# Token order, block products for one more feed-forward unit, and the order of wide and narrow matmuls in a two-layer encoder

## The chip, the cores and the metric

The kernel runs on one core of one Trainium2 chip. The metric is device microseconds of one execution; lower is better. The engines are named as in the profile: PE (TensorE, matmuls), PEld (its weight loads), DVE (VectorE), ACT (ScalarE), POOL (GpSimd) and SP (SyncE, which issues most DMAs). The kernel was run three times, and one further execution was profiled.

## What is computed

Two layers of an encoder over 512 tokens (a grid of 8 rows by 64 columns) of width 1024. Each layer has a mixer (neighbourhood attention and grouped-query attention), a cross attention to 256 memory tokens, and the feed-forward part that the change is about:

```python
def conv_ffn(h, w_up, conv_w, conv_b, w_down):
    u = h @ w_up                                    # (512, 1024) @ (1024, 2 * 2816)
    up = jnp.pad(u, ((0, 0), (1, 1), (0, 0)))
    u = up[:, :-2] * conv_w[0] + up[:, 1:-1] * conv_w[1] + up[:, 2:] * conv_w[2] + conv_b
    gate, val = jnp.split(u, 2, axis=-1)
    return (jax.nn.silu(gate) * val) @ w_down

def reference(x, mem, ...):
    for l in range(DEPTH):                          # DEPTH = 2
        x = x + hybrid_mixer(rms_norm(x, norm_mix[l]), ...)
        x = x + memory_cross_attention(rms_norm(x, norm_mem_q[l]), rms_norm(mem, norm_mem_kv[l]), ...)
        x = x + conv_ffn(rms_norm(x, norm_ffn[l]), w_up[l], conv_w[l], conv_b[l], w_down[l])
    return rms_norm(x, norm_final)
```

The convolution runs over neighbouring positions in the reference's order of tokens, in which token 64 r + c is row r, column c of the grid.

## The kernel before

**Layout.** Activations lie transposed: 128 of the 1024 features on the partitions, 512 tokens along the free dimension, in eight chunks `xT[c]`. Tokens are kept column by column: token 8 c + r is row r, column c, so that a window of the neighbourhood attention is a run of tokens. The neighbour in the convolution then lies 8 places away, except at the seam from one row of the grid to the next.

**Precision.** Every float32 operand is split into a rounded part `hi` and a remainder `lo`, and a product of two is three matmuls (`mm3`, called by `gemm_T`): hi by hi, hi by lo, lo by hi. ACT makes `hi` and POOL or DVE `lo`, of the activations as of the weights (`emit_split`).

**Feed-forward.** A unit is 128 columns of gate and 128 of value; there are 22 per layer. A plain unit (`up_project`) is two sides of 8 chunks by 3 matmuls of 512 columns: 48 wide matmuls. The first `PLAIN` = 6 units are plain. The others (`up_forms`) use a scheme of seven block products in place of eight: the weights of gate and value as a 2 by 2 block matrix over halves of the features, the tokens as two halves of 256. The sums and differences of weight blocks are made ahead by DMAs that add in DRAM (`make_form`, for the groups of `SHARES_OF_FORMS`), those of tokens once per layer: `scale_tokens` writes the scaled tokens to SBUF, `token_sums` forms t1 to t4 from them, `split_form` rounds each form into hi and lo. In one product (`product`) each of four chunks takes two matmuls:

```python
PE.matmul(bank, wh[:, i], both, start=start and k == 0, stop=False, skip_group_check=True)
PE.matmul(bank[:, halves[0]], wl[:, i], both[:, halves[0]], start=False, stop=k == 3, skip_group_check=True)
```

The first is wide, 512 columns: 256 tokens of `hi` and beside them 256 of `lo`. The second is narrow: the 256 of `hi`. A unit of this kind is 28 wide and 28 narrow matmuls in three PSUM banks (`mm`, `tr`, `sc`); the halves of a bank are added afterwards on DVE, ACT and POOL. So plain units are bound to the operands `ffn.ops`, the others to `xform`; t3, b22 and t4 are written over `ffn.hi` and `ffn.lo` once the plain units have read them.

**After the matmuls** of a unit, `convolve` applies the three taps (ACT the middle one, DVE the two others, each in two pieces because of the seam), silu and the product, and `split_psum` rounds the result, `acts[j]`. `GROUPS` puts the 22 units into four groups. The down projection of a group (`down`) has 8 rows of 3 matmuls per unit; its rows are placed between the products of the next group's units by `sequence`, one or two per unit. The last group's is done by `down_closing` (layer 0) or `down_last` (layer 1, with the final norm and the output).

**Order.** The program is recorded first, and a planner (`Order`) then fixes the order on PE, DVE, ACT and POOL from its own table of costs, with a search by a fixed seed. PE may be moved ahead of the written order where a matmul's operands are planned to be late. SP keeps the written order. Buffers are handed out from pools: 21 general tiles `r`, 14 temporaries `t`, PSUM banks `mm` 4, `sc` 2, `tr` 2, and two large tiles `xg` for a normalised operand.

In the rows of the profile the sides of plain units are 24 matmuls of 128x512 in a row into `mm` or `sc` with `xg` as input; a product is eight matmuls, 128x512 and 128x256 in turn, with `r` or `xg` as the tokens' form; a row of the down projection is 15 or 18 matmuls of 128x512 into `mm` with `r` as input. A few matmul records can be missing from a trace.

Of the kernel before, what the change touches and what calls it, by code (L numbers as in the profile page):

```python
# [19 lines left out]
P = 128  # L20
S = 512
# [4 lines left out]
NB = S // P  # L26
KC = D // P
# [5 lines left out]
GROUPS = [(0, 6), (6, 6), (12, 5), (17, 5)]  # L33
# [5 lines left out]
PLAIN = 6  # L39
SHARES_OF_FORMS = [(6, 4), (10, 4), (14, 4), (18, 4)]  # L40
# [50 lines left out]
class Counted(Free):  # L91
# [4 lines left out]
    def matmul(self, out, lhsT, rhs, **k):  # L96
        n = 1
        for d in rhs.shape[1:]:
            n *= d
        self.ns += max(107.0, (n + 32) / 2.4)  # L100
        return self.engine.matmul(out, lhsT, rhs, **k)  # L101

# [581 lines left out]
def encoder_kernel(ctx: ExitStack, tc: tile.TileContext, t: dict, out: bass.AP):  # L684
# [151 lines left out]
    def sequence():  # L836
# [4 lines left out]
        for g, (j0, nj) in enumerate(GROUPS):  # L841
            row = 0
            for j in range(j0, j0 + nj):
                to = 0 if g == 0 else min(KC, 2 * (j - j0) + 1) if j < j0 + nj - 1 else KC
                rows, row = range(row, to), to
                if j < PLAIN:
                    yield "up", j, None
                    continue
# [149 lines left out]
    def row_rep(rstd, n, tag, bufs, copy):  # L998

        pr = row_bank(rstd, n)  # L1000
        rep = tpool.tile([P, n * P], F32, tag=tag, name=nm(tag), bufs=bufs)
        copy(rep, pr[:, : n * P])
        return rep, pr[:, : n * P]

    class Norm:
# [11 lines left out]
        def close(self, c, pm):  # L1017


            DVE.tensor_add(pm, pm, xT[c])  # L1020
            DVE.tensor_copy(xT[c], pm)
            self.operand(c, src=pm)
            self.square(c)

        def operand(self, c, act=ACT, src=None, dve=DVE, hi_only=False, lo_only=False):
# [3 lines left out]
            e = None if lo_only else act.activation(hi, src, AF.Copy, scale=g)  # L1029
# [44 lines left out]
        def spread(self, copy=ACT.copy):  # L1074
            self.rep, self.psum = row_rep(self.rstd, self.n // P, "rep", 1, copy)
# [122 lines left out]
    for l in range(DEPTH):  # L1198
# [641 lines left out]
        ffn = nn  # L1840
        acts = {}

        def up_project(j, side):
            pm = ps_s() if side else ps_mm()
            gemm_T(pm, get_w(("up", j, side)), ffn.ops, range(KC), 0, KC - 1)
            return pm

        def up_first():
# [3 lines left out]
            for side in range(2):  # L1852
                ws.append(get_w(("up", 0, side)))
                us.append(ps_mm())
                gemm_T(us[side], ws[side], ffn.ops, range(KC - 1), 0, KC - 1)
            for side in range(2):
                gemm_T(us[side], ws[side], ffn.ops, [KC - 1], 0, KC - 1)
# [16 lines left out]
        def convolve(j, us):  # L1874
            cs = []
            for side in range(2):
# [31 lines left out]
        def scale_tokens():  # L1908
# [3 lines left out]
            for c in range(KC):  # L1912
                DVE.scalar_tensor_tensor(xn[c // 2][:, c % 2], xT[c], ffn.gain(c), ffn.psum, op0=ALU.mult, op1=ALU.mult)

        def token_sums():


            for name, a, b in (("t1", (0, 1), (0, 0)), ("t2", (1, 1), "t1"), ("t3", (1, 1), (0, 1)), ("t4", (1, 0), "t2")):
                raw = raw_forms[name] = rtile((4, HALF), F32)
                for i in range(2):  # L1920
                    k = slice(2 * i, 2 * i + 2)
                    one, other = quarter(*a)[i], raw_forms[b][:, k] if isinstance(b, str) else quarter(*b)[i]
                    if name == "t4":
                        POOL.tensor_add(raw[:, k], one, other)
                    elif name == "t2":
                        DVE.tensor_sub(raw[:, k], other, one)
                    else:
                        (POOL if name == "t3" else DVE).tensor_sub(raw[:, k], one, other)

        def split_form(name, where=None):  # L1930
# [4 lines left out]
            for i, v in enumerate(place):  # L1935
                hi, lo = (v[:, :, half] for half in halves)
                src = quarter(*direct[name])[i] if name in direct else raw_forms[name][:, 2 * i : 2 * i + 2]
                if name in ("t1", "t4"):
                    ACT.mul(hi, src, -1.0)
                    DVE.scalar_tensor_tensor(lo, src, -1.0, f(hi), op0=ALU.mult, op1=ALU.subtract)  # L1940
                else:
                    ACT.copy(hi, src)
# [281 lines left out]
```

## Time and profile before

| | |
|---|---|
| median of 3 runs | 1304.17 us (1303.88 to 1304.24) |
| the profiled execution | 1304.26 us, of which the span from first to last instruction 1302.5 |
| ACT, share of the span | 60% |
| POOL, share of the span | 66% |
| weight loads on PE, share of the span | 84% |
| HBM read, written | 218.45 MB, 69.21 MB |

A page of the profile shows for each engine the time in which it was busy, and the chain of work that ended last, followed back from the last instruction. A row of that chain is a start, a duration, an engine, the tile written, the line and a count. The list of waits has, for an engine and a line, what ended its idle time, the total, the times and the longest. A row of the timeline is a start, the time until the end, an engine, a line, an operation with output and inputs, its size and a count; since matmuls are pipelined, each lasts longer than the distance from its start to the next one's, and that distance is what it costs. Rows of groups end with busy time and mean duration (ns), then idle time before. Rows of a stretch have, per engine (PE, PEld, DVE, ACT, POOL), busy time and count, then the granted clock, the DMA share and GB/s.

### The profile page before, as it was taken

Reading aid. Unit: us, or ns where it says so; the run is one execution under the profiler, and the core shown is the slowest. Engines: PE = TensorE matmul, PEld = TensorE weight load, DVE = VectorE, ACT = ScalarE, POOL = GpSimd, SP = SyncE. Lnnn points to the kernel's source line nnn. Section 1 sums busy time; section 2 is a strip of 40 time slices with the busy share of each in tenths; the row PEclk is TensorE's granted clock in tenths of the full one; section 3 lists DMA queues with packets and bytes.
Section 4 is the critical chain, followed back from the end, with each engine's and each line's share of the span. In section 5 each row is a group of like instructions: output and inputs, shape, how many; then the busy total and the mean of one; then the engine's idle time right before and its main releaser. Section 6 shows DMA issues by size and latency. Waiting matters only on the chain.

```text
span 1302.5 us, 19581 instructions
## 1 busy us (share of the span) xinstructions
PE 1292.3 (99%) x6699; PEld 1096.4 (84%) x6699; DVE 916.0 (70%) x1869; ACT 776.6 (60%) x1463; POOL 857.7 (66%) x650
## 2 busy tenths in 40 slices
PE   9999999999999999999999999999999999999997
PEld 8888888888888888888888888888888888888887
DVE  6559877665996685676735698776759966666675
ACT  6667866565564554454636687775645545545454
POOL 3657966728667776776746579766466766767673
PEclk9999999999999999999999999999999999999999
DMA  9734599597787789687555435986872454555541
GB/s 289 211 108 121 160 262 203 168 211 199 186 192 204 207 230 234 189 234 212 157 152 172 144 84 185 253 191 214 186 170 85 130 158 134 163 157 150 149 138 65
DMA packets 287426, 229.68 MB, mean 176 GB/s; under 512 B 7648, under 2 KB 243680, under 8 KB 287328
## 3 DMA queue, kind: packets, MB, share of 16 engines
q1 hardware_dynamic: 270016, 194.49, 49.7%
q0 software_dynamic: 16896, 33.56, 14.6%
q8 instruction: 53, 0.87, 0.3%
q10 hardware_dynamic: 416, 0.39, 0.1%
q14 instruction: 45, 0.37, 0.1%
HBM read 218.45 MB, written 69.21 MB: 221 GB/s over the span
## 4 chain that ended last, share of the span: by engine, by line
PE 95%; DVE 3%; ACT 1%; issue 1%; POOL 0%; POOLq 0%; DVEq 0%; ACTq 0%
PE mm L101 69%; PE sc L101 18%; PE tr L101 4%; PE tr L1586 2%; PE tr L1431 1%; PE tr L1780 1%; DVE t L1891 0%; DVE r L1080 0%; DVE sc L1403 0%; PE tr L1501 0%; DVE r L1129 0%; DVE t L1456 0%; DVE t L1489 0%; ACT r L1079 0%; ACT t L1409 0%
## 5 line engine op out<-in xcount | busy, mean ns | idle before, releaser
L790 POOL TENSOR_TENSOR lo<-raw,hi 128x512 fp32r<-128x512 f32 (+3 forms) x325 | 567.0, 1761 | 280.6 <-ACT hi L789 224.1
L789 ACT CAST hi<-raw 128x1024 fp32r<-128x1024 f32 (+3 forms) x361 | 287.8, 814 | 274.4 <-issue 71.3
L101 PE MATMUL mm<-r,hi 128*128 128x512 f32 (+1 forms) x1344 | 432.8, 390 | 0.0
L101 PEld LDWEIGHTS mm<-r,hi 128*128 128x128 f32 x1344 | 246.4, 188 | 49.8
L101 PE MATMUL mm<-r,lo 128*128 128x512 f32 (+1 forms) x832 | 286.5, 347 | 0.0
L101 PE MATMUL mm<-xg,hi 128*128 128x512 f32 x800 | 262.2, 394 | 0.6 <-DVE t L1963 0.6
L101 PE MATMUL mm<-xg,lo 128*128 128x512 f32 (+1 forms) x528 | 177.9, 337 | 0.0
L101 PEld LDWEIGHTS mm<-r,lo 128*128 128x128 f32 x832 | 156.4, 188 | 22.6 <-POOL lo L790 0.5
L101 PEld LDWEIGHTS mm<-xg,hi 128*128 128x128 f32 x800 | 148.6, 188 | 31.9 <-DVE t L1963 1.0
L101 PE MATMUL sc<-xg,hi 128*128 128x512 f32 x352 | 116.3, 395 | 0.0
L101 PE MATMUL mm<-hi,xg 128*128 128x512 f32 (+1 forms) x384 | 111.2, 360 | 0.0
L101 PEld LDWEIGHTS mm<-xg,lo 128*128 128x128 f32 x528 | 99.4, 188 | 12.2
L1086 POOL TENSOR_SCALAR t<-t,s 128x512 f32<-128x512 f32 (+1 forms) x112 | 67.2, 623 | 45.6 <-DVE s L1570 22.2
L101 PE MATMUL sc<-xg,lo 128*128 128x256 f32 (+1 forms) x240 | 79.4, 332 | 0.0
L1982 POOL TENSOR_TENSOR t<-t 128x256 f32<-128x256 f32 x32 | 42.4, 1324 | 56.1 <-ACT t L1981 55.2
L101 PEld LDWEIGHTS sc<-xg,hi 128*128 128x128 f32 x352 | 66.1, 189 | 14.5 <-ACT xg L78 0.4
L101 PEld LDWEIGHTS mm<-hi,xg 128*128 128x128 f32 x384 | 68.0, 189 | 9.1 <-DVE r L1280 0.2
L101 PE MATMUL sc<-r,r 128*128 128x256 f32 (+1 forms) x352 | 74.4, 330 | 0.0
L1989 DVE TENSOR_TENSOR sc<-mm,t 128x256 f32<-128x256 f32 x32 | 13.8, 433 | 79.2 <-ACT t L1988 79.2
L101 PE MATMUL sc<-r,hi 128*128 128x512 f32 x192 | 68.7, 398 | 0.0
L101 PE MATMUL mm<-lo,xg 128*128 128x512 f32 (+1 forms) x192 | 68.6, 357 | 0.0
L790 DVE TENSOR_TENSOR lo<-raw,hi 128x1024 fp32r<-128x1024 f32 (+1 forms) x36 | 44.2, 1229 | 33.8 <-ACT hi L789 33.5
(222 smaller groups left out, 2438.3 us busy)
## 6 DMA issues: line engine op xcount, KB each, us to landing
raw<-in_w_up SPq DMA_DIRECT2D x56, 512.0 KB, 4.5
dr_sums<-in_w_up SPq DMA_DIRECT2D x16, 1024.0 KB, 8.0
dr_diffs<-in_w_up SPq DMA_DIRECT2D x16, 1024.0 KB, 7.6
raw<-dr_sums SPq DMA_DIRECT2D x32, 512.0 KB, 4.1
raw<-dr_diffs SPq DMA_DIRECT2D x32, 512.0 KB, 4.1
raw<-in_w_in SPq DMA_DIRECT2D x25, 512.0 KB, 4.8
raw<-in_w_down SPq DMA_DIRECT2D x32, 384.0 KB, 3.7
raw<-in_w_mem_kv SPq DMA_DIRECT2D x16, 512.0 KB, 4.4
```

The costliest lines, as they stand in the source:

```text
L101: return self.engine.matmul(out, lhsT, rhs, **k)
L789: act.copy(hi[:, k], raw[:, k])
L790: (POOL if eng[0] == "P" else DVE).tensor_sub(lo[:, k], raw[:, k], f(hi)[:, k])
L1086: eng.tensor_scalar(e, e, sums[:, col : col + 1], 1.0, op0=ALU.mult, op1=ALU.mult)
L1431: PE.transpose(tr[:, (2 * i + c) * P : (2 * i + c + 1) * P], es[j][:, i, c * P : (c + 1) * P], ident)
L1586: PE.transpose(tr[:, k * P : (k + 1) * P], es[j][:, k * P : (k + 1) * P], ident)
L1780: PE.transpose(tr[:, (2 * c + i) * P : (2 * c + i + 1) * P], e[:, i, c * P : (c + 1) * P], ident)
L1982: POOL.tensor_add(vc, vc, u2)
L1989: DVE.tensor_add(ch, ah, l4)
```

## The change

It has five parts.

- Tokens lie in another order outside the feed-forward part: in blocks of 8 columns, in each block row by row. Token 64 a + 8 b + e is column 8 a + e of row b. A block of 128 tokens still holds 16 columns, so the attention's windows stay. Input layout, rotary tables and bias tables follow on the host. In the feed-forward part tokens lie in the reference's order, row by row. `crossed` and `runs` are the two views of one tile with the three indices a, b, e; going from one order to the other swaps a and b and keeps runs of 8 tokens.
- So the plain units' matmuls read `ffn.ops` through `crossed` (`by_row`), and every place that passes between the two orders does so in its views: `row_rep`, `scale_tokens`, `down`, `close`, `operand`, and `down_last`, which adds into new tiles `z`. The convolution's outer taps are one operation of 511 columns each instead of one of 504 and one of 7.
- `PLAIN` is 5: unit 5 is made by block products. The groups of the down projection are 5, 6, 6, 5 units and the shares of the weight forms 4, 4, 4, 5.
- `token_sums` writes t1 and t2 to PSUM banks `tr` and rounds them from there; t4's sum goes from POOL to DVE. `scale_tokens` takes the gain on ACT and the norm on DVE.
- In `product` the four wide matmuls come first, then the four narrow ones.

```diff
-GROUPS = [(0, 6), (6, 6), (12, 5), (17, 5)]
+GROUPS = [(0, 5), (5, 6), (11, 6), (17, 5)]
-PLAIN = 6
-SHARES_OF_FORMS = [(6, 4), (10, 4), (14, 4), (18, 4)]
+PLAIN = 5
+SHARES_OF_FORMS = [(5, 4), (9, 4), (13, 4), (17, 5)]
...
+def runs(v):
+
+    return v.rearrange("p (a b e) -> p a b e", a=GROUPS_OF_COLS, b=ROWS)
+
+
+def crossed(v):
+
+    return v.rearrange("p (a b e) -> p b a e", a=ROWS, b=ROWS)
...
+        by_row = [tuple(map(crossed, v)) for v in ffn.ops]
...
-            gemm_T(pm, get_w(("up", j, side)), ffn.ops, range(KC), 0, KC - 1)
+            gemm_T(pm, get_w(("up", j, side)), by_row, range(KC), 0, KC - 1)
...
-                for wi, dst, src in (
-                    (w[0], slice(8, S), slice(0, S - 8)),
-                    (w[0], slice(1, 8), slice(S - 8, S - 1)),
-                    (w[2], slice(0, S - 8), slice(8, S)),
-                    (w[2], slice(S - 8, S - 1), slice(1, 8)),
-                ):
+                for wi, dst, src in ((w[0], slice(1, S), slice(0, S - 1)), (w[2], slice(0, S - 1), slice(1, S))):
...
-                DVE.scalar_tensor_tensor(xn[c // 2][:, c % 2], xT[c], ffn.gain(c), ffn.psum, op0=ALU.mult, op1=ALU.mult)
+                v = xn[c // 2][:, c % 2]
+                ACT.activation(runs(v), crossed(xT[c]), AF.Copy, scale=ffn.gain(c))
+                DVE.tensor_mul(runs(v), runs(v), crossed(ffn.psum))
...
+            for i in range(2):
+                k = slice(2 * i, 2 * i + 2)
+                t1, t2 = (ps_t().rearrange("p (k n) -> p k n", k=2) for _ in range(2))
+                DVE.tensor_sub(t1, quarter(0, 1)[i], quarter(0, 0)[i])
+                DVE.tensor_sub(t2, t1, quarter(1, 1)[i])
+                halves_of("t2", i, t2, False, DVE)
+                DVE.tensor_add(raw_forms["t4"][:, k], t2, quarter(1, 0)[i])
+                halves_of("t1", i, t1, True, DVE)
+                POOL.tensor_sub(raw_forms["t3"][:, k], quarter(1, 1)[i], quarter(0, 1)[i])
...
+                both = [xform[form][k // 2][:, k % 2] for k in range(4)]
                 for k in range(4):
-                    i = 4 * part + k
-                    both = xform[form][k // 2][:, k % 2]
-                    PE.matmul(bank, wh[:, i], both, start=start and k == 0, stop=False, skip_group_check=True)
-                    PE.matmul(bank[:, halves[0]], wl[:, i], both[:, halves[0]], start=False, stop=k == 3, skip_group_check=True)
+                    PE.matmul(bank, wh[:, 4 * part + k], both[k], start=start and k == 0, stop=False, skip_group_check=True)
+                for k in range(4):
+                    PE.matmul(bank[:, halves[0]], wl[:, 4 * part + k], both[k][:, halves[0]], start=False, stop=k == 3,
+                              skip_group_check=True)
...
-                DVE.tensor_add(xT[m], xT[m], pm)
+                DVE.tensor_add(runs(xT[m]), runs(xT[m]), crossed(pm))
...
-                nn.close(m, pm)
+                nn.close(m, pm, True)
```

How the order changes is seen at three places. The names in the rows are tiles with a running number; a row is a line, an operation, output and inputs, a size and, where equal rows follow each other, a count.

PE, the first unit by block products in layer 0, its second product (gate weights, form b21), before. Here that is unit 6, `tr` is the bank, `r` the form, `hi` and `lo` the weights:

```order
L101 MATMUL tr_4054<-r_3681,hi_3959 128x512
L101 MATMUL tr_4054<-r_3681,lo_3960 128x256
L101 MATMUL tr_4054<-r_3681,hi_3959 128x512
L101 MATMUL tr_4054<-r_3681,lo_3960 128x256
L101 MATMUL tr_4054<-r_3682,hi_3959 128x512
L101 MATMUL tr_4054<-r_3682,lo_3960 128x256
L101 MATMUL tr_4054<-r_3682,hi_3959 128x512
L101 MATMUL tr_4054<-r_3682,lo_3960 128x256
```

PE, the same place of the change, now unit 5, from the end of the last plain side (`sc_3902`, unit 4) through the first row of the down projection (`mm_4043`):

```order
L102 MATMUL sc_3902<-xg_2894,lo_3825 128x512
L102 MATMUL mm_3960<-r_3675,hi_3872 128x512 x2
L102 MATMUL mm_3960<-r_3676,hi_3872 128x512 x2
L102 MATMUL mm_3960<-r_3675,lo_3873 128x256 x2
L102 MATMUL mm_3960<-r_3676,lo_3873 128x256 x2
L102 MATMUL tr_3961<-r_3681,hi_3872 128x512 x2
L102 MATMUL tr_3961<-r_3682,hi_3872 128x512 x2
L102 MATMUL tr_3961<-r_3681,lo_3873 128x256 x2
L102 MATMUL tr_3961<-r_3682,lo_3873 128x256 x2
L102 MATMUL sc_3962<-r_3770,hi_3903 128x512
L102 MATMUL mm_3960<-r_3768,hi_3903 128x512 x2
L102 MATMUL mm_3960<-r_3769,hi_3903 128x512 x2
```

Wide and narrow no longer alternate: four wide, then four narrow. One wide matmul of the product into `sc_3962` (form t1) now stands ahead of the product with form t2.

DVE, the convolution of unit 2 in layer 0, before (`mm_3689` is the gate's bank, `sc_3720` the value's, `t` the accumulators; L1913 is `scale_tokens`):

```order
L1891 SCALAR_TENSOR_TENSOR t_3753<-mm_3689,par,t_3753 128x7
L1913 SCALAR_TENSOR_TENSOR r_3665<-xT_99,par,tr_3587 128x512
L1891 SCALAR_TENSOR_TENSOR t_3753<-mm_3689,par,t_3753 128x504
L1891 SCALAR_TENSOR_TENSOR t_3759<-sc_3720,par,t_3759 128x504
L1891 SCALAR_TENSOR_TENSOR t_3759<-sc_3720,par,t_3759 128x7
L1891 SCALAR_TENSOR_TENSOR t_3753<-mm_3689,par,t_3753 128x7
L1891 SCALAR_TENSOR_TENSOR t_3759<-sc_3720,par,t_3759 128x504
L1891 SCALAR_TENSOR_TENSOR t_3759<-sc_3720,par,t_3759 128x7
```

And DVE in the change, the same unit's taps, between them the multiplications by the norm (L1932), behind them the second subtraction of the token differences (L1945):

```order
L1908 SCALAR_TENSOR_TENSOR t_3753<-mm_3689,par,t_3753 128x511
L1932 TENSOR_TENSOR r_3657<-r_3657,tr_3587 128x512
L1908 SCALAR_TENSOR_TENSOR t_3757<-sc_3720,par,t_3757 128x511
L1908 SCALAR_TENSOR_TENSOR t_3753<-mm_3689,par,t_3753 128x511
L1932 TENSOR_TENSOR r_3658<-r_3658,tr_3587 128x512
L1908 SCALAR_TENSOR_TENSOR t_3757<-sc_3720,par,t_3757 128x511
L1932 TENSOR_TENSOR r_3658<-r_3658,tr_3587 128x512
L1911 TENSOR_TENSOR mm_3689<-mm_3689,t_3757 128x512
L1945 TENSOR_TENSOR tr_3773<-tr_3772,r_3657 128x512
```

The short pieces of seven columns are gone, and the subtraction reads and writes PSUM banks.

More of the change, by code (lines that the diff above doesn't have):

```diff
@@ L847, in sequence @@
                     yield "up", j, None
+                    if rows:
+                        yield "down", g - 1, rows
                     continue
@@ L1015, in gain, with close, operand @@
             return par[:, self.l, self.gcol + c : self.gcol + c + 1]
[L1017 to L1022, printed above, removed]
+        def close(self, c, pm, by_row=False):
+            if by_row:
+                DVE.tensor_add(runs(pm), runs(pm), crossed(xT[c]))
+                DVE.tensor_copy(runs(xT[c]), crossed(pm))
+            else:
+                DVE.tensor_add(pm, pm, xT[c])
+                DVE.tensor_copy(xT[c], pm)
+            self.operand(c, src=pm, by_row=by_row)
             self.square(c)
-        def operand(self, c, act=ACT, src=None, dve=DVE, hi_only=False, lo_only=False):
+        def operand(self, c, act=ACT, src=None, dve=DVE, hi_only=False, lo_only=False, by_row=False):
             src = xT[c] if src is None else src
@@ L1934, in split_form @@
             direct = {"b11": (0, 0), "b21": (1, 0), "b22": (1, 1)}
-            for i, v in enumerate(place):
-                hi, lo = (v[:, :, half] for half in halves)
+            for i in range(len(place)):
                 src = quarter(*direct[name])[i] if name in direct else raw_forms[name][:, 2 * i : 2 * i + 2]
[L1938 to L1942, printed above, removed]
-                    (POOL if name == "b22" else DVE).tensor_sub(lo, src, f(hi))
+                halves_of(name, i, src, name == "t4", POOL if name == "b22" else DVE)
         def up_forms(j):
@@ L2027, in down_last @@
                 gemm_T(pm, w, list(parts[0].values()), range(LAST[0][1]), 0, LAST[0][1] - 1, slice(P * (m % 2), P * (m % 2) + P))
-                DVE.tensor_add(xT[m], xT[m], pm)
+                DVE.tensor_add(runs(z[m]), crossed(xT[m]), runs(pm))
+                xT[m] = z[m]
             js, ws = list(parts[1]), {}
@@ L2222 @@
     y = np.concatenate([y[0].reshape(D, HALF).T, y[1].reshape(HALF, D)])
[L2223 removed]
+    return np.ascontiguousarray(y).reshape(1, S, D)
```

58 lines of the change are left out of this document (31 added, 27 removed).

## Prediction

> **What bounds the kernel now.** I read the page first, then what TensorE waits for, then the chain that ended last, stage by stage, then the spacing of matmuls in the timeline.
>
> ```profile
> span 1302.5 us, 19581 instructions
> ...
> PE 1292.3 (99%) x6699; PEld 1096.4 (84%) x6699; DVE 916.0 (70%) x1869; ACT 776.6 (60%) x1463; POOL 857.7 (66%) x650
> ...
> PEclk9999999999999999999999999999999999999999
> ```
>
> TensorE is busy 99% of the span at full clock. Matmuls are pipelined, so this alone doesn't say that it is never held up; the list of its waits does.
>
> ```profile
> PE tr L101 <- POOL ident masks.py:199: 1.4, 1, 1.4
> PE tr L1431 <- DVE r L1297: 0.8, 1, 0.8
> PE mm L101 <- DVE t L1963: 0.6, 1, 0.6
> PE mm L101 <- DVE t L1457: 0.4, 2, 0.2
> PE tr L101 <- DVE r L1080: 0.3, 1, 0.3
> ```
>
> These are all: 3.5 us, of which 1.4 is the start. So the time is the number of matmuls times their spacing, plus a head and a tail that the change leaves alone. Whatever VectorE, ScalarE or GpSimd save can return at most 2.1 us. The spacing is read from the chain:
>
> ```profile
> 343.05 5.44 PE sc L101 x24
> 348.49 5.44 PE mm L101 x24
> ...
> 402.32 1.41 PE tr L101 x8
> 403.73 2.83 PE mm L101 x16
> 406.56 1.41 PE sc L101 x8
> 407.97 5.54 PE mm L101 x26
> 413.51 1.41 PE sc L101 x8
> ```
>
> The first two rows are the sides of a plain unit: 24 wide matmuls (512 columns) in 5.44 us, 0.2267 each. The x8 rows are block products of later units: four wide and four narrow (256 columns), alternating, 1.41 us. The x26 row is one product and 18 wide matmuls of a down row: 5.54 - 1.41 = 4.13 us, where 18 x 0.2267 is 4.08. So a row behind products costs 0.05 more than its matmuls.
>
> **Part 1, unit 5 by block products.** It removes, per layer, two sides of 24 wide matmuls, 2 x 5.44 = 10.88 us, and adds 7 products. At 1.41 these would take 9.87: a gain of 1.01 per layer, 2.0 in all. The order of part 2 makes each cheaper.
>
> **Part 2, wide products first.** How do four wides behind four narrows run? Before has no such pattern in a row, but it has runs of narrow matmuls followed by wide ones, of two kinds:
>
> ```profile
> 43.44 1.12 PE L101 MATMUL sc<-r,r 128*128 128x256 f32 x8
> 44.39 0.63 PE L101 MATMUL mm<-xg,hi 128*128 128x512 f32 x2
> 44.86 0.39 PE L101 MATMUL mm<-xg,lo 128*128 128x512 f32 x1
> 45.09 0.63 PE L101 MATMUL mm<-xg,hi 128*128 128x512 f32 x2
> 45.55 0.39 PE L101 MATMUL mm<-xg,lo 128*128 128x512 f32 x1
> 45.78 0.62 PE L101 MATMUL mm<-xg,hi 128*128 128x512 f32 x2
> ...
> 917.91 0.63 PE L101 MATMUL sc<-r,r 128*128 128x256 f32 x4
> 918.38 0.40 PE L101 MATMUL mm<-r,hi 128*128 128x512 f32 x1
> 918.61 1.30 PE L101 MATMUL mm<-r,r 128*128 128x512 f32 x5
> 919.75 0.39 PE L101 MATMUL mm<-r,hi 128*128 128x512 f32 x1
> ```
>
> Start to start (the first column), eight narrows take 0.95 us, four 0.475. In the first kind the next three wides take 0.70 and the three after them 0.69, not 0.68: four are 0.93, a product 1.405. In the second kind four narrows take 0.47, the first wide 0.23 and the five after it 1.14 (0.228 each): four are 0.914, a product 1.384. So a product costs 1.384 to 1.405; I take the middle, 1.395, since nothing says which kind recurs. Against 1.41 that is 0.015 (0.005 to 0.026) less, times the 224 products that exist (16 units x 7 x 2 layers): 3.4 us (1.1 to 5.8). This charges the slow wides to the run of narrows ahead of them, so the 0.05 on a down row is already in it; some 20 rows per layer stand behind products (24 less those that follow a row): 40 x 0.05 = 2.0 us more. Unit 5 at 1.395 gives 10.88 - 9.77 = 1.11 per layer, 2.2 in all (2.1 to 2.4). **Sum: 3.4 + 2.0 + 2.2 = 7.6 us, from 5.2 to 10.2.**
>
> **Part 3, tokens in blocks of 8.** The 480 plain matmuls that remain (5 units x 48 x 2) now stream tokens in 64 runs of eight, where they streamed one run of 512. Before has no such operand. The nearest is the neighbourhood values product (L1453), whose moving operand is two pieces 512 elements apart:
>
> ```profile
> 66.31 1.11 PE L101 MATMUL mm<-r,r 128*128 128x256 f32 x8
> 67.27 0.40 PE L101 MATMUL mm<-hi,xg 128*128 128x512 f32 x1
> ```
>
> Eight of them take 0.96 us, eight one-piece matmuls 0.95. At the resolution of the rows a hop costs 0 to about 1 ns. A gain has no source, since a run of 512 is already paced like its columns. 63 hops x 480 matmuls x 1 ns would be 30 us at the far end; I take 0, where the row lies. [...]
>
> VectorE and ScalarE now read or write in the same runs, and some of VectorE's reads are of PSUM. VectorE already reads PSUM with a hop at every element:
>
> ```profile
> L1963 DVE TENSOR_REDUCE t<-mm 128x256 f32<-128x512 f32 x64 | 44.0, 688 | 17.8 <-PE mm L101 17.5
> L1999 DVE TENSOR_TENSOR xT<-xT,mm 128x512 f32<-128x512 f32 x48 | 32.8, 683 | 8.9 <-PE mm L101 8.9
> L1891 DVE SCALAR_TENSOR_TENSOR t<-tr,par,t 128x7 f32<-128x7 f32 x64 | 13.8, 215 | 0.0
> ...
> L1891 DVE SCALAR_TENSOR_TENSOR t<-sc,par,t 128x7 f32<-128x7 f32 x20 | 4.3, 213 | 0.0
> ```
>
> Its 512 elements take 688 ns hopping and 683 straight, so I add nothing. ScalarE has no such row; its crossed passes (8 per layer among the plain units, 8 where layer 0 closes its rows) stand at places where nothing waits for ScalarE now, so I add 0 there too, and one slot of its length, some 0.6 us, if the last of them showed. The last two rows are the first and last of four groups, 176 operations on seven columns; all of them go, 176 x 0.214 = 38 us of VectorE. TensorE does not wait for them, so I credit 0; at most the 2.1 us above.
>
> **Part 4, differences through PSUM.** Two subtractions and their roundings read or write PSUM, one sum moves from GpSimd to VectorE, and the scaled tokens cost ScalarE eight extra passes per layer. The cover is the plain stage, now one unit shorter:
>
> ```profile
> 321.00:370.00 49.00, 49.00 (x219) 40.59 (x218) 47.13 (x72) 27.27 (x40) 30.21 (x17) 1.00 0.83 205
> 366.30 2.19 ACT L1942 CAST xg<-r 128x512 fp32r<-128x512 f32 x4
> 368.16 3.45 POOL L1943 TENSOR_TENSOR xg<-r,xg 128x512 fp32r<-128x512 f32 x2
> ```
>
> In the first row VectorE (third pair) is busy 47.1 of 49 us, and TensorE still loses nothing. After it the stage has 10.9 us less of TensorE. VectorE loses a unit's convolution (two multiplications, four long taps, four short, product and rounding, some 2 x 0.69 + 4 x 0.73 + 4 x 0.21 + 2 x 0.69 = 6.5 us) and about 4 x 0.85 us of short taps in the others, which leaves 47.1 - 6.5 - 3.4 = 37.2 us for a stage of 38.1: as full as before, and no fuller. ScalarE (27.3 of 49 us) has room for eight more passes of 2.19 / 4 = 0.55 us. What could come late is the last forms for unit 5 (the next two rows, their casts and GpSimd's rounding, from 366.30 to 371.61 or 5.3 us). In the new order TensorE has four products and three wide matmuls ahead of their first use, 4 x 1.395 + 0.68 = 6.3 us. It fits, by little. I add 0. DMA gains 0.75 MB per layer of loads and one unit's sums and differences, made long before; the share in that stage is 0.83, and no wait of TensorE is for a load.
>
> The profiled execution took 1304.26 us, 1.76 more than its span, and 0.09 more than the median of the runs. 1304.26 - 7.6 = **1296.7 us**, 0.6% faster. A measurement of this kernel can tell about 0.2%, 2.6 us, from no change.
>
> **Rivals.**
> *Reading in runs slows TensorE (slower).* Mechanism: each new run of eight costs the moving stream one column's time, 5.44 / 24 / 512 = 0.44 ns. Place: the ten plain units. Price: 63 x 0.44 = 28 ns x 480 = 13.4 us, so 1296.7 + 13.4 = 1310.1. It decides from 7.6 / 480 = 16 ns per matmul, 0.25 ns per hop. Against it: the two-piece operand runs as fast as the one-piece one. For it: one hop tests little. [...]
> *The order of wide and narrow is worth nothing.* If each product still takes 1.41 and rows keep their 0.05, only unit 5 gains: 1304.26 - 2.0 = 1302.2. Against it: both kinds of run above.
> *The last forms come late.* If GpSimd's 3.45 us stood bare in both layers: 1296.7 + 6.9 = 1303.6; half of it, 1300.1. Against it: a stage as full lost nothing before.
> *The change doesn't do what it says.* The new program could break up the groups of four; its order on TensorE keeps nearly all, so this has no chance of its own.
>
> **How the numbers follow.** Forecast 0.68 (own range 1294.0 to 1299.0, from 10.2 and 5.2); order worth nothing 0.09; late forms 0.09; slow reads 0.14. The range of 8 in 10 takes in the first three: low 1294.0, high 1303.0. It leaves out the slow reads (0.14) and the worst of the late forms. Faster by over 0.2% (below 1301.6): the forecast and most of the late forms, 0.75. Within: order worth nothing and the rest, 0.11. Slower: slow reads, 0.14.
>
> **What would show it.** Parts 1 and 2: x8 rows of the chain near 1.40 and down rows near 4.08; if they are 1.41 and 4.13, the order is worth nothing. Part 3: the plain sides, x24, stay at 5.44; at 6.1 the slow reads hold, and the forecast is wrong. Part 4: TensorE's waits stay near 3.5 us, none on the forms of unit 5. VectorE's busy time falls by 35 to 45 us without a trace in the span.

## The result, and the profile after

The change takes **1316.78 us** (median of 4 runs, 1315.77 to 1319.1) against 1304.11 of the kernel before beside it: a ratio of 1.0098, 95% interval 1.0086 to 1.0111. It is 1% slower, where 0.6% faster was forecast, and it lies outside the forecast range of 1294.0 to 1303.0. The profiled execution took 1317.39 us, 13.1 more than the one of before. Two executions of runs further down, 4941 us in e1_sorted and 2160 us in e6_six, were slow ones and are left out of the ratios, though counted in the number of runs.

The page of the profile after, its span and engines:

```profile
span 1315.6 us, 19500 instructions
...
PE 1304.3 (99%) x6715; PEld 1098.0 (83%) x6715; DVE 907.6 (69%) x1711; ACT 790.3 (60%) x1489; POOL 859.7 (65%) x652
```

TensorE is busy for the same share as before and at full granted clock (0.999 over the span), but for 12 us more. The list of what TensorE waits for, after (total, times, longest), the first five rows:

```profile
PE tr L102 <- POOL ident masks.py:199: 1.4, 1, 1.4
PE tr L1452 <- DVE r L1318: 0.8, 1, 0.8
PE mm L102 <- DVE sc L2009: 0.5, 1, 0.5
PE mm L102 <- DVE t L1988: 0.4, 1, 0.4
PE tr L1607 <- DVE r L1318: 0.4, 1, 0.4
```

With four more of 0.2 to 0.3 these are 4.5 us, 1.0 more than before. So nearly all of the loss lies in the spacing of the matmuls, not in waits. Below is the chain that ended last, after, at the plain stage of layer 0 and in the stage of block products (start, duration, engine, tile, line, count):

```profile
295.75 18.96 PE mm L102 x81
...
315.49 7.19 PE mm L102 x27
...
323.57 6.31 PE sc L102 x24
329.88 6.32 PE mm L102 x24
...
361.48 6.32 PE sc L102 x24
...
398.34 1.40 PE tr L102 x8
399.74 2.81 PE mm L102 x16
402.55 1.41 PE sc L102 x8
403.95 4.81 PE mm L102 x23
```

Of the entry of the plain stage the prediction showed no rows. In before they are:

```profile
294.94 18.36 PE mm L101 x81
...
314.08 6.29 PE mm L101 x27
```

A side of a plain unit takes 6.32 us in place of 5.44, that is 0.263 per matmul in place of 0.227. The products are at 1.40, near the forecast. The x23 row is one product and 15 matmuls of a down row, which take 3.41, or 0.227 each, so in this row the surplus of a down row is nearly gone. The plain stage thus became slower and the stage of block products quicker. In the plain stage of one layer the two long runs at the entry take 0.60 and 0.90 us more than before, and the seven sides after them 0.875 each, together 7.6 us. Layer 1 shows the same, so it is **15.2 us in all**. Against that stands what the order of products saves, 3.0 us (worked out under e2_wide). These two give +12.2 us where the medians differ by +12.7, which leaves nothing of the 2.2 us that unit 5 was to bring.

The timeline of after in a side (start, time until the end, engine, line, operation, size, count) shows the slow spacing directly:

```profile
331.30 0.68 PE L102 MATMUL mm<-xg,hi 128*128 128x512 f32 x2
331.82 0.43 PE L102 MATMUL mm<-xg,lo 128*128 128x512 f32 x1
332.09 0.68 PE L102 MATMUL mm<-xg,hi 128*128 128x512 f32 x2
332.60 0.44 PE L102 MATMUL mm<-xg,lo 128*128 128x512 f32 x1
```

From start to start, three matmuls take 0.79 us, where three straight ones take 0.68.

### The profile page after: what moved, and what is told of

The parts are those of the page before. It is cut to its first block, busy times and chain, and to the rows that moved or that the text cites. A ratio compares the mean times of both kernels' runs of the same rounds, so it can differ in the third digit from the quotient of the medians.

```text
span 1315.6 us, 19500 instructions
## 1 busy us (share of the span) xinstructions
PE 1304.3 (99%) x6715; PEld 1098.0 (83%) x6715; DVE 907.6 (69%) x1711; ACT 790.3 (60%) x1489; POOL 859.7 (65%) x652
## 3 DMA queue, kind: packets, MB, share of 16 engines
q0 software_dynamic: 16896, 35.65, 15.2%
## 4 chain that ended last, share of the span: by engine, by line
PE 92%; DVE 3%; DMA 1%; ACT 1%; POOL 1%; issue 1%; SPq 0%; POOLq 0%; ACTq 0%; DVEq 0%
PE mm L102 66%; PE sc L102 18%; PE tr L102 4%; PE tr L1607 2%; DMA raw<-in_w_up 1%; PE tr L1452 1%; POOL lo L801 1%; PE tr L1801 1%; DVE sc L1424 0%; DMA raw<-in_w_in 0%; DVE r L1101 0%; ACT hi L800 0%; PE tr L1522 0%; DVE t L1908 0%; DVE r L1150 0%
## 5 line engine op out<-in xcount | busy, mean ns | idle before, releaser
L801 POOL TENSOR_TENSOR lo<-raw,hi 128x512 fp32r<-128x512 f32 (+3 forms) x327 | 574.0, 1774 | 285.4 <-ACT hi L800 235.3
L102 PE MATMUL mm<-r,hi 128*128 128x512 f32 (+1 forms) x1360 | 414.9, 389 | 0.4 <-DVE t L1988 0.4
L102 PE MATMUL mm<-r,lo 128*128 128x512 f32 (+1 forms) x848 | 259.0, 346 | 0.0
L102 PE MATMUL mm<-xg,hi 128*128 128x512 f32 x784 | 238.5, 400 | 0.5 <-DVE sc L2009 0.5
L102 PE MATMUL mm<-xg,lo 128*128 128x256 f32 (+1 forms) x528 | 146.3, 340 | 0.0
L102 PEld LDWEIGHTS mm<-xg,lo 128*128 128x128 f32 x528 | 90.3, 190 | 18.1
L102 PE MATMUL sc<-xg,hi 128*128 128x512 f32 x328 | 102.0, 410 | 0.2 <-ACT hi L79 0.2
L1100 ACT CAST r<-tr 128x512 fp32r<-128x512 f32 x82 | 47.3, 587 | 43.0 <-DVE tr L1911 32.2
L801 DVE TENSOR_TENSOR lo<-raw,hi 128x1024 fp32r<-128x1024 f32 (+1 forms) x38 | 54.9, 1446 | 25.5 <-ACT hi L800 25.5
L1101 DVE TENSOR_TENSOR r<-tr,r 128x512 fp32r<-128x512 f32 x82 | 55.7, 686 | 13.3 <-ACT r L1100 9.7
```

The costliest lines, as they stand in the source:

```text
L801: (POOL if eng[0] == "P" else DVE).tensor_sub(lo[:, k], raw[:, k], f(hi)[:, k])
L1100: ACT.copy(hi, ps)
L1101: DVE.tensor_sub(lo, ps, f(hi))
```

## The experiments

Two theories stood at first. **Reads:** TensorE streams an operand that lies in 64 runs of eight more slowly, and that is the whole loss. **VectorE:** the plain stage, one unit shorter, no longer covers VectorE's work, so that TensorE is held up behind it. In the diffs below, what is left out is as in the kernel named first.

**e1_sorted: the change with straight reads.** The step from one order to the other is made when the cross attention closes a chunk, by VectorE and ScalarE, and TensorE reads straight rows. With it the views in the other places of the feed-forward part go straight again, and `scale_tokens` is one operation on VectorE as in before, without ScalarE's extra passes; the diff leaves these out.

```diff
+            by_row = by_row or self.gcol == G_FFN
+            DVE.tensor_add(pm, pm, xT[c])
             if by_row:
-                DVE.tensor_add(runs(pm), runs(pm), crossed(xT[c]))
                 DVE.tensor_copy(runs(xT[c]), crossed(pm))
...
-        by_row = [tuple(map(crossed, v)) for v in ffn.ops]
+        by_row = ffn.ops
```

> The change, but tokens pass to row order where the feed-forward part is entered (VectorE writes xT and ScalarE writes hi in row order), so that no moving operand of TensorE is in pieces; nothing else of the change is undone. Theory A (TensorE pays about 36 ns for each of the 480 matmuls that read 64 runs of eight): the plain sides go from 6.32 back to 5.44 us, and the time from 1317 to 1300 (1298 to 1302), below the kernel before. Rival B (the loss comes from the planner's other order, fuller engines and late operands, and the slow sides only take up slack): sides at 5.44, but the time stays above 1308.

Measured: 1303.63 us (11 runs), ratio to the kernel before 0.9997 (0.9988 to 1.0006). The sides are back at 5.44, and 13.2 us came back, as much as the whole loss. The time is above the 1298 to 1302 expected and below the rival's 1308. That it isn't faster than before has a cause of its own, in the list of waits and the timeline of VectorE:

```profile
PE mm L102 <- DVE lo L801: 1.8, 1, 1.8
...
PE mm L102 <- DVE xg L1052: 0.8, 1, 0.8
```

```profile
375.74 3.41 DVE L801 TENSOR_TENSOR lo<-raw,hi 128x1024 fp32r<-128x1024 f32 x1
379.08 0.68 DVE L2022 TENSOR_TENSOR xT<-xT,mm 128x512 f32<-128x512 f32 x1
```

The plain stage ends at 360.2 us. When TensorE comes to the sums of unit 6, at 377 us, VectorE is still at the remainder of their weights, and TensorE starts again at 379.21. The granted clock behind this wait is 0.50 (379.9 to 381.6 us), so the loss is larger than 1.8 us.

**e2_wide: the kernel before with only the wide matmuls first.**

> The kernel before with one edit: in a block product the four wide matmuls first, then the four narrow ones. By the prediction: 3.4 + 2.0 = 5.4 us less, 1298.7. By the trace of the change (a product 1.40 us in place of 1.41, and nearly every run of wides still slow at its start): 2 to 3 us less, 1301.7. If the order is worth nothing: 1304.

Measured: 1304.16 us (11 runs), ratio 0.9999 (0.999 to 1.0008): no gain in the time. To see the order's own part, I took the distances between starts in the two stages of block products, less 226.7 ns for each wide and 120 for each narrow matmul on record, and set apart the long ones (over 290 and 160 ns). Before has some 3.6 us left over per layer, e2_wide and the change 2.0 to 2.1. So the order is worth 1.5 us per layer, 3.0 in all. In e2_wide this is lost again elsewhere: the long distances in the same two stages grow by some 1.4 us, with the largest waits on VectorE's remainders (0.9 and 0.7 us), and the stretch with the mixer and the cross attention of layer 1, which the edit does not touch, takes 301.7 us (660.4 to 962.1) in place of 300.6 (661.5 to 962.1).

**e3_unit5: the kernel before with only unit 5 by block products.**

```diff
-GROUPS = [(0, 6), (6, 6), (12, 5), (17, 5)]
+GROUPS = [(0, 5), (5, 6), (11, 6), (17, 5)]
-PLAIN = 6
-SHARES_OF_FORMS = [(6, 4), (10, 4), (14, 4), (18, 4)]
+PLAIN = 5
+SHARES_OF_FORMS = [(5, 4), (9, 4), (13, 4), (17, 5)]
```

> The kernel before with unit 5 of each layer by block products and groups of 5, 6, 6, 5; wide and narrow still alternate, tokens as before. By the sum of the prediction: 2.0 us less, 1302.2. Rival: the forms for unit 5 come late, or the plain stage, one unit shorter, can't cover VectorE: 1304 or more, and a wait of TensorE just behind the plain stage.

Measured: 1329.71 us (5 runs, 1328.0 to 1331.7), ratio 1.0195 (1.0181 to 1.0209), 25 us slower. Below are the first rows of its list of waits, and a stretch that takes in the plain stage of layer 0 and 5 us behind it (busy time and count of PE, PEld, DVE, ACT, POOL):

```profile
PE sc L101 <- DVE lo L790: 7.2, 5, 2.3
PE mm L101 <- DVE t L1963: 6.7, 3, 2.8
PE mm L101 <- ACT t L1884: 2.3, 1, 2.3
```

```profile
321.00:365.00 44.00, 41.75 (x192) 34.56 (x191) 42.26 (x63) 25.96 (x40) 28.69 (x15) 1.00 0.66 170
```

VectorE is busy 42.3 of 44 us, 96%, the same share as before (47.1 of 49). Up to the end of the plain stage, from 321 to 359 us, it is busy 36.3 of 38, and TensorE loses nothing there; its first wait follows at 362.7. So the share of busy time did not tell the two cases apart. And the wait for ScalarE's L1884 is paid for twice, by its own length and by slow matmuls behind it. Below are the timeline behind this wait, and the granted clock of two stretches (the number before the last two):

```profile
364.90 0.47 PE L101 MATMUL mm<-r,hi 128*128 128x512 f32 x1 [2.25 <-ACT t L1884]
365.21 0.36 PE L101 MATMUL mm<-r,lo 128*128 128x256 f32 x1
365.38 0.63 PE L101 MATMUL mm<-r,hi 128*128 128x512 f32 x1
365.81 0.41 PE L101 MATMUL mm<-r,lo 128*128 128x256 f32 x1
```

```profile
364.90:367.30 2.40, 2.40 (x8) 2.06 (x9) 2.40 (x3) 1.16 (x2) 1.39 (x1) 0.57 1.07 291
370.00:380.00 10.00, 9.75 (x52) 7.97 (x51) 10.00 (x24) 4.97 (x8) 2.99 (x3) 1.00 0.94 264
```

After 2.25 us without work a wide matmul takes 0.43 us in place of 0.23, at a granted clock of 0.57 in this stretch. From 370 to 380 us the clock is at 1.00.

**e4_pieces: the change with other pieces per side.** The tokens of units 1 to 4 are read in runs of e, with hops of b times e, so that these units' outputs are not the reference's.

```diff
+            b, e = tried[j, side]
+            return [tuple(v.rearrange("p (a b e) -> p b a e", b=b, e=e) for v in pair) for pair in ffn.ops] if b > 1 else ffn.ops
```

> The change, with the moving operand of the plain units 1 to 4 read in another pattern on each side: straight, and runs of 1, 2, 4, 8, 16, 32, 64 and 128 elements, with different distances; the tokens of these units come out in a wrong order, the number of matmuls is the same. Read is the time of a side (24 matmuls; 5.44 straight, 6.32 in runs of eight, hops of 64). Theory A1 (a price per hop, 36.6 / 63 = 0.58 ns): runs of 16 give 5.87, of 32 5.65, of 4 7.2, of 2 8.9, whatever the distance. Theory A2 (any operand in pieces is slow): all at 6.3. Theory A3 (the distance of the hops decides): sides with runs of eight but hops of 16, 32 or 256 elements differ from each other.

Measured: 1315.39 us (one execution). Below is the chain of layer 0; the sides are, in this order, (b, e) = (8, 2), (8, 4), (8, 8), (8, 16), (8, 32), (2, 8), (32, 8):

```profile
322.62 10.35 PE sc L102 x24
332.97 5.93 PE mm L102 x24
338.89 6.11 PE sc L102 x24
345.01 5.58 PE mm L102 x24
350.58 5.67 PE sc L102 x24
356.25 5.60 PE mm L102 x24
361.85 5.84 PE sc L102 x24
```

64 runs of eight cost 0.16, 0.40 or 0.67 us per side more than 5.44 where the next run lies 16, 256 or 64 elements on, and 0.09 in layer 1, where it lies 32 on (5.53). Twice as many pieces, runs of four, cost 0.15 in layer 1 (5.59, hops of 8) and 0.49 here. Runs of 16 and 32 cost 0.14 to 0.31. Pieces of 64 and 128 (layer 1) cost nothing that shows. Runs of two, and in layer 1 of one (10.34), take nearly twice as long. So there is no fixed price per hop and none per operand in pieces. Whether the distance of the hops decides, as the third theory says, is not shown: each pattern was run on one or two sides, and e7_modes shows that the side before has a part in it. The low speed of runs of two is not the clock, which is granted in full while the 24 matmuls of that side run:

```profile
323.00:332.00 9.00, 9.00 (x23) 4.28 (x22) 5.78 (x9) 2.96 (x5) 2.09 (x1) 1.00 1.04 231
```

**e5_pool: e1_sorted with one load taken off VectorE.** GpSimd makes the remainders of the sums' weights of units 5 and 6, on which e1_sorted waited 1.8 us.

```diff
-            cols(("sums", j), made[l][g][0], 0, KC, P * (j - j0), P, "D")
+            cols(("sums", j), made[l][g][0], 0, KC, P * (j - j0), P, "P" if j < PLAIN + 2 else "D")
```

> As e1, but GpSimd in place of VectorE makes the remainders of the sums' weights of units 5 and 6. Theory: in e1 TensorE's wait of 1.8 us for VectorE's remainder just behind the plain stage of layer 0, and the 1.0 us of half-clock matmuls behind it, are what is left between 1303.6 and 1300.8; they go, and the time is 1300.8 (1300 to 1302). Rival: the wait moves to another late operand: 1303 or more.

Measured: 1312.69 us (5 runs), ratio 1.0061 (1.0049 to 1.0073). That wait is gone, and others take its place, 2.9 us on the roundings of the last forms (L1953), 1.7 and 1.0 at the entry (L1052, L1047), 1.0 on ScalarE. The rival held: the wait moves on, and the new order is worse.

**e6_six: e1_sorted with six plain units and the old groups.**

> As e1, but unit 5 stays plain (groups 6, 6, 5, 5 as before): row order, two long taps, differences through PSUM and wide products first, without the sixth unit of block products. Theory: wide first gives 1.5 us per layer (debt of the products 3.6 to 2.1), no new wait at the end of the plain stage, since VectorE has a unit more of cover: 1301.3 (1300.3 to 1302.5). So unit 5 with its waits is worth nothing against e1's 1303.6, rather costs 2. Rival: 1303.6 or more, so that e1's rest is due to the row order or the differences.

Measured: 1303.79 us (12 runs), ratio 0.9996 (0.9988 to 1.0005). No wait at the end of the plain stage; what remains is 1.4 us on VectorE's remainder L1052 and 0.9 on ScalarE's L1047, both where the feed-forward begins. The rival held here, and unit 5, which was expected to cost e1_sorted 2 us, makes no difference that shows.

**e7_modes: the change with straight and crossed sides in turn.** Only the tokens' order in the reads is changed, so units 1 to 4 are again not the reference's.

```diff
+            which = tried.get((j, side), "hl")
+            return [tuple(crossed(v) if n in which else v for n, v in zip("hl", pair)) for pair in ffn.ops]
```

> The change, with the plain sides of units 1 to 4 reading straight or in runs of eight (hops of 64) by turns, and in some sides only hi or only lo in runs; the tokens of these units come out in a mixed order, the number of matmuls is the same. Read is the time of a side of 24. Theory M1 (a side in runs can stand in a quick or a slow state, which it takes over from what ran before): in runs directly behind a straight side 5.60, the state of unit 0 (0.233 each), not 6.32. Theory M2 (the slow state belongs to units 1 to 4): 6.32 wherever both operands are in runs. Only lo in runs (a third of the matmuls): 5.73 if each pays alone; only hi: 6.03.

Measured: 1307.32 us (one execution). Three sides from its chain: the second of two crossed sides in layer 0, the straight side behind it, and a crossed one in layer 1:

```profile
329.24 6.21 PE mm L102 x24
335.45 5.45 PE sc L102 x24
...
978.60 5.60 PE sc L102 x24
```

In the same program a side is quick when its reads are straight (5.45 to 5.49). Summed over all sides, those of this run take 10.0 us less than those of the change, and its span is 10.1 us shorter. So the reads are shown as the cause with everything else in place. Sides in which only lo is crossed, a third of the matmuls, take 5.71 and 5.76, and the one in which only hi is, two thirds, 5.76 where 6.03 was expected: the price does not go by the number of crossed matmuls. In layer 1 a crossed side behind a straight one, and its continuation, look like this in the timeline:

```profile
973.31 0.63 PE L102 MATMUL mm<-xg,hi 128*128 128x512 f32 x2
973.79 0.43 PE L102 MATMUL mm<-xg,lo 128*128 128x512 f32 x1
974.05 0.69 PE L102 MATMUL mm<-xg,hi 128*128 128x512 f32 x2
...
976.33 0.64 PE L102 MATMUL mm<-xg,hi 128*128 128x512 f32 x2
976.80 0.40 PE L102 MATMUL mm<-xg,lo 128*128 128x512 f32 x1
977.03 0.64 PE L102 MATMUL mm<-xg,hi 128*128 128x512 f32 x2
```

Three matmuls take 0.71 to 0.79 us for the first five triples and 0.70 from then on; the side as a whole takes 5.90. The next two crossed sides stay at 0.70, which makes 5.60. In layer 0, where the first crossed side follows the small matmuls of the norm, two crossed sides take 6.18 and 6.21. The same reads at the same hops thus run at two speeds, 0.233 and up to 0.263 us per matmul, and keep the one they are in from one side to the next. What sets the speed stays open. The change runs at the slower one from unit 1 on.

**e8_seed: the kernel before with another seed of the planner's search** (4 to 7), all else kept.

> The kernel before with another seed of the planner's search and nothing else. Theory: another order with the same work moves the time by 1 to 2 us either way through waits of its own (1302.5 to 1306), which is the size of e2's lost gain. Rival: within 0.3 us of 1304.3, so that e2's new waits belong to the edit.

Measured: 1306.24 us (10 runs), ratio 1.0014 (1.0006 to 1.0023). Another order alone moves 2 us, through waits of its own: 0.9 on L1080 and 0.7 on the remainders. The stretch with the mixer and the cross attention of layer 1 takes 301.8 us here and 300.6 before. Differences of this size between two programs need not be due to their edit.

**e9_psum: the kernel before with wide first and with t1 and t2 through PSUM.** `token_sums`, `split_form` and `product` are those of the change; tokens, taps, `scale_tokens` and six plain units are as before.

> The kernel before with wide products first and the differences t1, t2 through PSUM; tokens, taps and six plain units as before. Theory: wide first is worth 3.0 us (1.5 per layer, as measured in the forms' stages), and in e2_wide the new waits for VectorE's remainders (lo) took them back; with t1, t2 in PSUM VectorE has less to do before the forms, so those waits shrink: 1300.5 to 1302.5. Rival: the waits come from the planned order and not from VectorE's load, so others take their place: 1303.5 to 1304.5, with PE's waits for VectorE and ScalarE at 3 us or more.

Measured: **1302.2 us** (11 runs), ratio 0.9985 (0.9976 to 0.9994). The waits are 3.4 us. Of the 3.0 us 2.1 are seen in the time, though a difference of this size alone would prove little (e8_seed).

**e10_psum5: e9_psum with unit 5 by block products.**

> e9_psum with unit 5 by block products as well (groups 5, 6, 6, 5). Theory: the 25 us that unit 5 cost alone (e3_unit5) were VectorE's differences falling behind in a plain stage one unit shorter; through PSUM most of that goes: 1300 to 1309, with less than 5 us of waits behind the plain stages. Rival: it is the eight taps in pieces and the rounding of the weights that fill VectorE there, and the differences matter little: 1318 to 1328, the waits of e3_unit5 still there.

Measured: 1308.34 us (8 runs, 1305.03 to 1310.68), ratio 1.0031 (1.002 to 1.0041). The same edit that cost 25 us alone costs 6.1 here. So the two edits of e9_psum take most of the trouble of e3_unit5 away. That it is the differences is likely, since VectorE is busy 43.7 us of the stretch from 321 to 370 in e9_psum and 47.1 before, but no run has them without wide first. Unit 5 still costs, and saves nothing.

**e11_slow6: the change with six plain units and the old groups**, crossed reads and all else kept.

> The change with six plain units and the old groups, all else kept (slow reads too). Theory: 96 more plain matmuls at the slow 263 ns instead of 227 cost 3.5 us, and unit 5 no longer saves its 2.2: about 1322, range 1320 to 1324. Rival: in the change unit 5 by block products costs as much as it saves, or more, because VectorE runs late behind the plain stage: 1315 to 1319.

Measured: 1320.48 us (4 runs), ratio 1.0125 (1.0109 to 1.014). This is 3.7 more than the change. The two sides that are added per layer read crossed too; the last of layer 0 is

```profile
373.53 6.32 PE sc L102 x24
```

and the four together hold 4 x 0.88 = 3.5 us of slow reads. So unit 5 by block products is worth 0.2 us, not 2.2, in the change (the intervals leave some 2 us either way). And the sum closes: 15.2 + 3.5 = 18.7 us of slow reads less 3.0 for the order is 15.7, measured 16.1.

**e12_entry: e6_six with another closing.** The sum goes in row order into a bank of `tr`; the copy, the rounding and the remainder read it there.

```diff
-            DVE.tensor_add(pm, pm, xT[c])
             if by_row:
-                DVE.tensor_copy(runs(xT[c]), crossed(pm))
+                ordered = ps_t()
+                DVE.tensor_add(runs(ordered), crossed(pm), crossed(xT[c]))
+                pm = ordered
             else:
-                DVE.tensor_copy(xT[c], pm)
-            self.operand(c, src=pm, by_row=by_row)
+                DVE.tensor_add(pm, pm, xT[c])
+            DVE.tensor_copy(xT[c], pm)
+            self.operand(c, src=pm)
```

> e6_six with the sum at the closing put in row order into a bank of tr, so that the copy to xT, the rounding and the remainder all read one ordered PSUM tile, as in the kernel before, and the remainder no longer reads xT from SBUF. Theory: in e6_six the remainders L1052 that read SBUF took 2.5 and 2.95 us beside POOL where the kernel before takes 0.74 from PSUM, and this is what PE waited for at the feed-forward's entry (1.4 + 0.9 us and the half clock behind them): those waits go, and what is left is wide first and the whole taps: 1299.5 to 1301.5. Rival: the sum through another bank makes the entry no quicker, since two banks of tr hold it up, or the planner puts the wait elsewhere: 1303 to 1306.

Measured: **1301.28 us** (11 runs, 1300.7 to 1301.87), ratio 0.9976 (0.9967 to 0.9985), the fastest of all. The group of VectorE's remainders (busy time, mean ns) in e6_six and then in e12_entry:

```profile
L1052 DVE SCALAR_TENSOR_TENSOR xg<-xT,par,xg 128x512 fp32r<-128x512 f32 x24 | 34.2, 1444 | 1.5 <-ACT xg L1047 1.5
```

```profile
L1054 DVE SCALAR_TENSOR_TENSOR xg<-tr,par,xg 128x512 fp32r<-128x512 f32 x24 | 17.6, 748 | 7.7 <-ACT xg L1052 7.6
```

Read from PSUM the operation takes half the time, and the waits at the entry are gone. The time is 0.9 us below e9_psum, which has neither the new token order nor the whole taps, and a seed alone moves more: what shows of the gain over before is about what the order of products is worth. This version keeps the new token order, the whole taps, the differences through PSUM and wide first, and leaves out the crossed reads and unit 5.

## Why the prediction was wrong, step by step

**Part 3 is the step that failed**: "63 hops x 480 matmuls x 1 ns would be 30 us at the far end; I take 0, where the row lies." The row was the neighbourhood values product, two pieces of 256 columns in all. e4_pieces shows that a few long pieces do cost nothing (straight speed at 128 elements) and that this says nothing of runs of eight: with the change's hops these cost 28 ns per matmul in that run and 263 - 227 = 36 in the change, 15.2 us in all where the sum had 0. The row bounded a price per hop, and there is no fixed price per hop. I had kept slow reads as a rival with a chance of 0.14, but placed the value on a row with 1 hop to stand for one with 63.

**The slow-reads rival** had the right place and nearly the right price: 13.4 us forecast, 15.2 measured, 1310.1 forecast for the time. Its mechanism, one column's time per run, is refuted: 64 runs cost 4 to 28 ns per matmul in e4_pieces, and the same 64 runs at the same hops 6 or 36 in e7_modes and the change. So the nearness of its price is luck. Its test, x24 rows at 6.1 in place of 5.44, told the cases apart (6.32). Its 1310.1 was 6.7 us short of the median: 1.8 for the price, most of the rest because it kept 7.6 us of gains, of which 3.0 came.

**Part 2** was right in mechanism and too large in size. Four wides in a row do gain, and the down rows lose part of their surplus. But its two terms were 3.4 + 2.0 = 5.4 us, and 3.0 were measured. In the timeline the stage after looks like this:

```profile
399.58 1.09 PE L102 MATMUL mm<-xg,hi 128*128 128x512 f32 x4
400.50 0.64 PE L102 MATMUL mm<-xg,lo 128*128 128x256 f32 x4
400.98 1.09 PE L102 MATMUL mm<-r,hi 128*128 128x512 f32 x4
```

Four wides take 0.92 to 0.93 us behind narrows in every product, four narrows 0.48: 1.40. Of the two kinds in the trace of before, the slow one is the one that recurs; the middle between them was a choice without a ground. I also took the 0.05 of a down row as going whole, as an addition to the products' gain.

**Part 1** counted its matmuls rightly (7 x 1.40 = 9.8 for 10.88). What went wrong is the cover, which Part 4 put at nothing. In the change unit 5 was worth 0.2 us (e11_slow6); alone it cost 25 (e3_unit5), and with the differences through PSUM and wide first 6.1 (e10_psum5).

**Part 4, the last forms**, "It fits, by little. I add 0": nearly so in the change, but by luck, because the slow reads stretched the stage. After, a plain stage lasts 63.9 us against 67.2 before, which is 3.3 less and not the 10.9 less that the step assumed. Even so the stages behind the two plain stages lose some 1.9 and 0.5 us to long distances between matmuls, where e11_slow6 has 0.25 in each; that is most of the 2.2 that unit 5 was to bring. The two new waits there, 0.4 and 0.5 us, are for VectorE's work on the products' banks (L1988, L2009), not for the forms. With straight reads and five units (e1_sorted) VectorE's work did not fit, and what came late was the remainder of a unit's weights. The premise, "as full as before, and no fuller", was right and proved nothing: e3_unit5 has 36.3 us of VectorE's work in 38 where the prediction had 37.2 in 38.1, and fails, since what decides is whether the operands and banks of the next units are ready when TensorE comes to them. The late-forms rival (up to 6.9 us) has the place but not the operand. Of e3_unit5's 21.2 us of waits, where before has 3.5, 7.2 are for remainders of weights, 6.7 for sums of banks and 1.0 for a form's rounding (L1940); with the lower clock behind long ones (the mean over the span is 0.993, before 0.999) they make 25 us.

**VectorE's busy time** fell by 8.4 us, not 35 to 45. All taps together fell from 146.1 to 127.3 us, by 18.9 and not 38. The 38 came from the mean duration of a short tap, 0.214 us, but operations overlap: in before's timeline the next one starts 0.13 to 0.14 us after a short tap does (330.09, 330.23 and 330.36 us). The remainders of weights that VectorE makes rose from 44.2 to 54.9, two more of them and 1.45 us each in place of 1.23; other groups rose and fell by less. **Waits** came to 4.5 us, near the forecast 3.5.

## What to carry to other kernels

Before an operand is given a new layout, look for a row that reads it with the same run length and the same hops; a row with one hop does not price 63, and where none exists, the far bound deserves more than a rest of the chance. Let VectorE or ScalarE do the reordering while they write an operand that TensorE then reads many times (a side went from 6.32 us back to 5.44 here), and from PSUM rather than from SBUF (748 ns in place of 1444 for a remainder here). A stage's share of busy time does not tell whether it can be shortened: follow the last operation that the next stage needs, and count a wait of two microseconds on TensorE at more than its length (behind 2.25 us a wide matmul took 0.43 us here in place of 0.23). When another order alone moves the time by 2 us, read a smaller gain from the rows that the edit should change, and not from the time.

## What the runs showed of the hardware

- Matmuls of 128x512 whose moving operand lies in runs of eight floats took 230 to 263 ns (e4_pieces, the change), in runs of one or two floats 431 (10.35 / 24), straight 227, all at the full granted clock (0.999 over the span in e4_pieces, the change and before).
- The same crossed reads ran at two speeds, 233 ns (e7_modes, layer 1) and up to 263 ns (the change), and kept the one they were in from one side to the next (5.60 and 5.60 us, 6.18 and 6.21 us in e7_modes). The cause was not found.
- After 2.25 us without work TensorE's granted clock was 0.57 from 364.9 to 367.3 us and 1.00 from 370 to 380 us (e3_unit5); after 1.82 us without work it was 0.50 from 379.9 to 381.6 us (e1_sorted).
- VectorE's remainder with both inputs in SBUF took 1444 ns on average (L1052 in e6_six; 0.73 to 2.95 us from 296 to 308 us) and 748 with one of them in PSUM (L1054 in e12_entry). In the change it took 752 to 1774 ns in the eight cases with both in SBUF and 745 to 758 in the 32 with one in PSUM (L1052), with GpSimd at work beside each of the 40. What makes the former longer was not shown: no run took GpSimd away.
